# Softmax over 4096 rows of 32768: the last two tiles' stores moved to SyncE's DMA queue, stores in whole rows

One core of one Trainium2 chip. The metric is the device time of one execution in microseconds (us); the profile's span, which begins with the first instruction, is some 2 us shorter.

## The reference

```python
logits: (16, 256, 32768) float32, temperature = 1.0
scaled = logits / temperature
scaled = scaled - scaled.max(axis=-1, keepdims=True)
exp_scaled = np.exp(scaled)
return exp_scaled / exp_scaled.sum(axis=-1, keepdims=True)
```

537 MB are read and 537 MB written, each once.

## The kernel before

Each row of 32768 is cut into two halves on two neighbouring partitions, so a tile is 128 x 16384 floats (8.39 MB, 64 KB per partition), and there are G = 64 tiles, numbered 0 to 63, in three buffers. Loads are issued by SyncE (`nc.sync`), stores by ScalarE (`nc.scalar`). Each has one hardware DMA queue of its own in the profile, q1 (SyncE) and q10 (ScalarE), with 536.9 MB each; I call them the rings. Both feed the same sixteen DMA engines: in the trace, rows of both stand back to back. A transfer of a tile is 128 rows, eight for each DMA engine. The code is shortened here; the whole kernel follows below.

```python
def load(t):
    n = _END if t in (0, G - 1) else _LOAD        # 4096 or 16384 columns
    for s in range(0, W, n):
        nc.sync.dma_start(out=buf[t % _BUFS][:, s : s + n], in_=x[...])

def store(t, a, b):
    n = _END if t >= G - _FINE_STORES else b - a  # _FINE_STORES = 3
    for s in range(a, b, n):
        nc.scalar.dma_start(out=o[...], in_=buf[t % _BUFS][:, s : s + n])

def normalise(t):
    for k in range(K):                            # pieces of the tile
        nc.vector.tensor_reduce(out=nm[:, k], in_=xc, op=max, negate=True)
        nc.scalar.activation(out=xc, in_=xc, func=Exp, bias=nm[:, k], accum_out=ssum[:, k])
    ...                                           # combine maxima and sums: f = factor of each piece
    for k in range(K):
        nc.vector.tensor_scalar_mul(...)          # part of the piece
        nc.scalar.activation(..., func=Copy, scale=f[:, k])   # the rest of it
        if t == G - 1:
            store(t, a, c)                        # last tile: four stores, as pieces are done
    if 0 < t < G - 1:
        store(t, 0, W)

for t in range(_BUFS):
    load(t)
for t in range(G):
    normalise(t)
    if t and t + _BUFS - 1 < G:
        load(t + _BUFS - 1)
```

The program order is kept. Waits are added when it is built: a buffer is reloaded only when its store has landed, and all transfers share eight completion semaphores in turn. So tile 63's load waits for tile 60's store, and a transfer can also wait for an earlier one that used its semaphore.

Of the kernel before, what the change touches and what calls it, by code (L numbers as in the profile page):

```python
# [1 line left out]

# [4 lines left out]


_SPLIT = 2
_BUFS = 3  # L10
_LOAD = 16384
_PIECES = (4096, 4096, 4096, 2048, 2048)
_ON_DVE = (4096, 4096, 2048, 0, 0)
_END = 4096
_END_ON_DVE = 2560
_FINE_STORES = 3
_SETS = 3


@with_exitstack  # L20
def kernel(
    ctx: ExitStack,
    tc: tile.TileContext,
    logits: bass.AP,
    temperature: bass.AP,
    out: bass.AP,
):
    nc = tc.nc
    inv_t = 1.0 / float(temperature)
    P = nc.NUM_PARTITIONS  # L30
    fp32 = mybir.dt.float32
    Exp = mybir.ActivationFunctionType.Exp
    Copy = mybir.ActivationFunctionType.Copy
    X = mybir.AxisListType.X
    A = mybir.AluOpType

    xf = logits.flatten_outer_dims()
    of = out.flatten_outer_dims()
    N, V = xf.shape
    W = V // _SPLIT  # L40
    assert sum(_PIECES) == W and len(_PIECES) == len(_ON_DVE)
    x = xf.rearrange("n (h v) -> (n h) v", h=_SPLIT)
    o = of.rearrange("n (h v) -> (n h) v", h=_SPLIT)
    G = N * _SPLIT // P
    assert G * P == N * _SPLIT
    n_rounds = _SPLIT.bit_length() - 1
    K = max(len(_PIECES), W // _END)

    pool = ctx.enter_context(tc.tile_pool(name="fixed", bufs=1))
    buf = [pool.tile([P, W], fp32, tag=f"x{b}", name=f"x{b}") for b in range(_BUFS)]  # L50
    widths = dict(nm=K, ssum=K, ee=K, f=K, ttj=K, nMh=2, Sh=2, rS=1)
    stat = [
        {
            k: pool.tile([P, w], fp32, tag=f"{k}{s}", name=f"{k}{s}")
            for k, w in widths.items()
        }
        for s in range(_SETS)
    ]

    def load(t: int) -> None:  # L60
        n = _END if t in (0, G - 1) else _LOAD
        for s in range(0, W, n):
            nc.sync.dma_start(  # L63
                out=buf[t % _BUFS][:, s : s + n],
                in_=x[t * P : (t + 1) * P, s : s + n],
            )

    def store(t: int, a: int, b: int) -> None:
        n = _END if t >= G - _FINE_STORES else b - a
        for s in range(a, b, n):  # L70
            nc.scalar.dma_start(  # L71
                out=o[t * P : (t + 1) * P, s : s + n],
                in_=buf[t % _BUFS][:, s : s + n],
            )

    def combine(v, op) -> None:
        for j in range(n_rounds):
            mask = [i ^ (1 << j) for i in range(32)]
            nc.vector.stream_shuffle(  # L79
                out=v[:, j + 1 : j + 2], in_=v[:, j : j + 1], mask=mask  # L80
            )
            nc.vector.tensor_tensor(  # L82
                out=v[:, j + 1 : j + 2],
                in0=v[:, j : j + 1],
                in1=v[:, j + 1 : j + 2],
                op=op,
            )

    def normalise(t: int) -> None:
        xs = buf[t % _BUFS]  # L90
        if t in (0, G - 1):
            sizes = [_END] * (W // _END)
            on_dve = [_END_ON_DVE] * len(sizes)
        else:
            sizes, on_dve = _PIECES, _ON_DVE
        K = len(sizes)
        at = [sum(sizes[:k]) for k in range(K)]
        st = stat[t % _SETS]
        nm, ssum, ee, f, ttj = (st[k][:, :K] for k in ("nm", "ssum", "ee", "f", "ttj"))
        nMh, Sh, rS = st["nMh"], st["Sh"], st["rS"]  # L100
        for k in range(K):
            xc = xs[:, at[k] : at[k] + sizes[k]]
            nc.vector.tensor_reduce(  # L103
                out=nm[:, k : k + 1], in_=xc, axis=X, op=A.max, negate=True
            )
            if inv_t != 1.0:
                nc.vector.tensor_scalar_mul(
                    out=nm[:, k : k + 1], in0=nm[:, k : k + 1], scalar1=inv_t
                )
            nc.scalar.activation(  # L110
                out=xc,
                in_=xc,
                func=Exp,
                bias=nm[:, k : k + 1],
                scale=inv_t,
                accum_out=ssum[:, k : k + 1],
            )
            if t == 1 and k == 0:

                store(0, 0, W)  # L120
        nc.vector.tensor_reduce(out=nMh[:, 0:1], in_=nm, axis=X, op=A.min)  # L121
        combine(nMh, A.min)
        nc.scalar.activation(  # L123
            out=ee, in_=nm, func=Exp, bias=nMh[:, n_rounds : n_rounds + 1], scale=-1.0
        )
        nc.vector.tensor_tensor_reduce(  # L126
            out=ttj,
            in0=ee,
            in1=ssum,
            scale=1.0,  # L130
            scalar=0.0,
            op0=A.mult,
            op1=A.add,
            accum_out=Sh[:, 0:1],
        )
        combine(Sh, A.add)
        nc.vector.reciprocal(out=rS, in_=Sh[:, n_rounds : n_rounds + 1])  # L137
        nc.vector.tensor_scalar_mul(out=f, in0=ee, scalar1=rS)  # L138
        for k in range(K):
            a, b, c = at[k], at[k] + on_dve[k], at[k] + sizes[k]  # L140
            if b > a:
                nc.vector.tensor_scalar_mul(  # L142
                    out=xs[:, a:b], in0=xs[:, a:b], scalar1=f[:, k : k + 1]
                )
            if c > b:
                nc.scalar.activation(  # L146
                    out=xs[:, b:c], in_=xs[:, b:c], func=Copy, scale=f[:, k : k + 1]
                )
            if t == G - 1:
                store(t, a, c)  # L150
        if 0 < t < G - 1:
            store(t, 0, W)

    with tc.manual_schedule():
# [8 lines that stand above are left out]
# [1 line left out]
_INS = ['logits', 'temperature']  # L164
_OUTS = [((16, 256, 32768), 'float32')]

_NUMBERS = {'temperature': 1.0}


# [26 lines left out]
```

## Time and profile before

| | before |
|---|---|
| time, median of three runs | 2496.59 us (2495.63 to 2496.76) |
| span of the profiled run | 2493.4 us |
| VectorE (DVE) / ScalarE (ACT) busy | 63% / 55% |
| moved by DMA | 1073.9 MB, 431 GB/s over the span |

The prediction shows the lines. "GB/s" and "DMA" give one entry for each fortieth of the span. In a chain, each line is start, duration and what ran. In a timeline, `[12.54 <-DMA ...]` is the idle time before the line and what ended it; ACTq and SPq are an engine's DMA-issuing instructions.

One reading goes beyond these views. For each transfer the trace also records sixteen completions, one for each DMA engine, and for each row the start and duration on its engine. They don't name the engine, but a row that follows another on its engine begins 3 to 4 ns before that one ends, so a chain of rows can be followed. I call the engine that completes last the **late engine**.

### The profile page before, as it was taken

What the parts mean: (1) busy time and instruction counts of PE and PEld (TensorE: products, weight loads), DVE (VectorE), ACT (ScalarE), POOL (GpSimd) and SP (SyncE); (2) the same over time, 40 slices, a digit from 0 to 9 for tenths busy, and PEclk for the clock granted to TensorE, in tenths of its full rate; (3) what the DMA queues carried; (4) which work ended last, traced back from release to release, by engine and by line L of the source; (5) the groups of instructions that cost most, each with busy time, mean ns of one, the idle gap of its engine ahead of it and who ended that gap; (6) DMA issues with size and microseconds to landing.
All of it is one profiled execution on the core that took longest, in us unless ns stands there. A gap on an engine that the chain in (4) does not pass through costs nothing.

```text
span 2493.4 us, 2622 instructions
## 1 busy us (share of the span) xinstructions
DVE 1575.8 (63%) x1216; ACT 1367.7 (55%) x895; POOL 0.2 (0%) x4
## 2 busy tenths in 40 slices
DVE  6575665766657666575665755657656566575665
ACT  6464645646556465464554645546455464554654
POOL 0000000000000000000000000000000000000000
DMA  9999999999999999999999999999999999999998
GB/s 421 433 424 436 435 437 424 436 434 437 424 436 435 437 424 436 433 428 435 434 430 433 434 436 427 433 436 431 429 435 437 423 435 437 427 431 437 425 429 379
DMA packets 20612, 1073.91 MB, mean 431 GB/s; under 512 B 2288, under 2 KB 2288, under 8 KB 2288
## 3 DMA queue, kind: packets, MB, share of 16 engines
q10 hardware_dynamic: 10512, 536.88, 49.9%
q1 hardware_dynamic: 10080, 536.88, 49.9%
q14 instruction: 20, 0.16, 0.0%
HBM read 536.87 MB, written 536.87 MB: 431 GB/s over the span
## 4 chain that ended last, share of the span: by engine, by line
DMA 75%; DVE 15%; ACT 9%; issue 0%; SPq 0%; DVEq 0%; ACTq 0%
DMA x<-in_logits_dram 38%; DMA out_dram<-x 37%; DVE nm L103 11%; ACT x L110 7%; DVE x L142 3%; ACT x L146 2%; DVE f L138 0%; SPq L63 0%; ACT ee L123 0%; DVE rS L137 0%; DVE Sh L82 0%; DVE ttj L126 0%; DVE Sh L79 0%; DVEq L191 0%; ACTq L71 0%
## 5 line engine op out<-in xcount | busy, mean ns | idle before, releaser
L103 DVE TENSOR_REDUCE nm<-x 128x1 f32<-128x4096 f32 x318 | 1117.5, 3579 | 678.0 <-DMA x<-in_logits_dram 678.0
L110 ACT ACTIVATE x<-x,nm 128x4096 f32<-128x4096 f32 x318 | 965.3, 3036 | 1026.2 <-DVE nm L103 1013.6
L146 ACT ACTIVATE x<-x,f 128x2048 f32<-128x2048 f32 (+1 forms) x194 | 371.2, 1975 | 75.4 <-DVE f L138 74.1
L142 DVE TENSOR_SCALAR x<-x,f 128x4096 f32<-128x4096 f32 (+2 forms) x194 | 372.2, 1975 | 2.5 <-DVE f L138 0.2
L126 DVE CUSTOM_DVE_ANT_0 ttj<-ee,ssum 128x5 f32<-128x5 f32 (+1 forms) x64 | 10.6, 166 | 203.0 <-ACT ee L123 203.0
L110 ACT ACTIVATION_READ_ACCUMULATOR x<-x,nm 128x1 f32 x318 | 59.2, 186 | 0.0
L123 ACT ACTIVATE ee<-nm,nMh 128x5 f32<-128x5 f32 (+1 forms) x64 | 18.1, 283 | 0.0
L138 DVE TENSOR_SCALAR f<-ee,rS 128x5 f32<-128x5 f32 (+1 forms) x64 | 14.8, 231 | 2.2
L137 DVE RECIPROCAL rS<-Sh 128x1 f32<-128x1 f32 x64 | 10.5, 164 | 2.2
L82 DVE TENSOR_TENSOR nMh<-nMh 128x1 f32<-128x1 f32 x64 | 10.2, 160 | 2.2
L82 DVE TENSOR_TENSOR Sh<-Sh 128x1 f32<-128x1 f32 x64 | 10.2, 159 | 2.2
L121 DVE TENSOR_REDUCE nMh<-nm 128x1 f32<-128x5 f32 (+1 forms) x64 | 10.1, 157 | 2.2
L79 DVE STREAM_SHUFFLE nMh<-nMh 128x1 f32<-128x1 f32 x64 | 9.7, 151 | 0.0
L79 DVE STREAM_SHUFFLE Sh<-Sh 128x1 f32<-128x1 f32 x64 | 9.7, 151 | 0.0
L110 ACT ACT_TABLE_LOAD x1 | 1.3, 1283 | 8.1 <-DMA x<-in_logits_dram 8.1
L126 DVE DVE_READ_ACCUMULATOR2_ANT Sh<- 128x1 f32 x64 | 5.3, 83 | 0.0
L79 DVE LOAD_MASK_SELECT Sh<-Sh x64 | 0.9, 14 | 2.8
L79 DVE LOAD_MASK_SELECT nMh<-nMh x64 | 0.9, 14 | 2.8
L177 POOL MEMSET const-bfloat16-1.0<- 128x1 bf16 x1 | 0.1, 101 | 0.0
L177 POOL MEMSET const-uint8-127<- 128x1 uint8 x1 | 0.1, 101 | 0.0
L177 POOL MEMSET const-float32-0.0<- 128x1 f32 x1 | 0.1, 98 | 0.2 <-issue 0.2
L177 POOL MEMSET const-float32-1.0<- 128x1 f32 x1 | 0.1, 98 | 0.0
## 6 DMA issues: line engine op xcount, KB each, us to landing
out_dram<-x ACTq DMA_DIRECT2D x12, 2048.0 KB, 19.3
x<-in_logits_dram SPq DMA_DIRECT2D x8, 2048.0 KB, 18.4
x<-in_logits_dram SPq DMA_DIRECT2D x62, 43.6
out_dram<-x ACTq DMA_DIRECT2D x61, 44.3
```

Of the source, the lines that this page charges most:

```text
L79: nc.vector.stream_shuffle(out=v[:, j + 1 : j + 2], in_=v[:, j : j + 1], mask=mask)
L82: nc.vector.tensor_tensor(out=v[:, j + 1 : j + 2], in0=v[:, j : j + 1], in1=v[:, j + 1 : j + 2], op=op,)
L103: nc.vector.tensor_reduce(out=nm[:, k : k + 1], in_=xc, axis=X, op=A.max, negate=True)
L110: nc.scalar.activation(out=xc, in_=xc, func=Exp, bias=nm[:, k : k + 1], scale=inv_t, accum_out=ssum[:, k : k + 1],)
L121: nc.vector.tensor_reduce(out=nMh[:, 0:1], in_=nm, axis=X, op=A.min)
L123: nc.scalar.activation(out=ee, in_=nm, func=Exp, bias=nMh[:, n_rounds : n_rounds + 1], scale=-1.0)
L126: nc.vector.tensor_tensor_reduce(out=ttj, in0=ee, in1=ssum, scale=1.0, scalar=0.0, op0=A.mult, op1=A.add, accum_out=Sh[:, 0:1],)
L137: nc.vector.reciprocal(out=rS, in_=Sh[:, n_rounds : n_rounds + 1])
L138: nc.vector.tensor_scalar_mul(out=f, in0=ee, scalar1=rS)
L142: nc.vector.tensor_scalar_mul(out=xs[:, a:b], in0=xs[:, a:b], scalar1=f[:, k : k + 1])
L146: nc.scalar.activation(out=xs[:, b:c], in_=xs[:, b:c], func=Copy, scale=f[:, k : k + 1])
L177: nc = _bacc.Bacc("TRN2", target_bir_lowering=False, num_devices=1)
```

## The change

The intent: the last load should not share DMA time with a store that is less urgent, ScalarE should not issue (and wait for) stores while its arithmetic is on the critical path, and stores should use the largest rows.

```diff
-_FINE_STORES = 3
 ...
     def store(t: int, a: int, b: int) -> None:
-        n = _END if t >= G - _FINE_STORES else b - a
-        for s in range(a, b, n):
-            nc.scalar.dma_start(
-                out=o[t * P : (t + 1) * P, s : s + n],
-                in_=buf[t % _BUFS][:, s : s + n],
-            )
+
+        engine = nc.sync if t >= G - 2 else nc.scalar
+        engine.dma_start(
+            out=o[t * P : (t + 1) * P, a:b], in_=buf[t % _BUFS][:, a:b]
+        )
```

In effect: tile 61's store becomes one 8 MB transfer on ScalarE's ring instead of four of 2 MB; tile 62's becomes one on SyncE's ring, behind tile 63's load; tile 63's four go to SyncE's ring. Nothing else changes.

## The prediction

> **What bounds the kernel now.** I read the page first (slices, chain of work that ended last), then the end of the span as chain, timeline and windows, because the change touches only the stores of the last three tiles. There are 64 tiles of 128 x 16384 floats (8.39 MB), numbered 0 to 63; three buffers.
>
> ```profile
> DMA  9999999999999999999999999999999999999998
> GB/s 421 433 424 436 435 437 424 436 434 437 424 436 435 437 424 436 433 428 435 434 430 433 434 436 427 433 436 431 429 435 437 423 435 437 427 431 437 425 429 379
> DMA 75%; DVE 15%; ACT 9%; issue 0%; SPq 0%; DVEq 0%; ACTq 0%
> ```
>
> The DMA engines are full in every slice but the last, and the chain is three quarters DMA. 1073.9 MB in 2493.4 us is 431 GB/s; from 100 to 2400 us the windows give 433 GB/s. Neither number of bytes nor middle changes, so all that can be won is idle time of the DMA engines at the end. The windows over the end (window, length, DVE busy, ACT busy, POOL busy, clock, DMA share, GB/s) show how much that is:
>
> ```profile
> 2460.00:2465.00 5.00, 0.00 (x0) 5.00 (x5) 0.00 (x0) 1.00 1.02 436
> 2465.00:2470.00 5.00, 0.98 (x8) 3.85 (x4) 0.00 (x0) 1.00 0.25 108
> 2470.00:2475.00 5.00, 5.00 (x4) 4.03 (x3) 0.00 (x0) 1.00 0.63 264
> 2475.00:2480.00 5.00, 0.83 (x1) 2.05 (x2) 0.00 (x0) 1.00 0.99 419
> ```
>
> From 2465 to 2475 the engines are idle for 5 x 0.75 + 5 x 0.37 = 5.6 us on average: tile 62's store is out and tile 63's is not yet ready. The chain and ScalarE's timeline name the cause:
>
> ```profile
> 2411.84 41.26 DMA x<-in_logits_dram
> 2453.10 0.02 issue
> 2453.12 0.02 ACTq L71
> ...
> 2453.18 0.34 ACTq L71
> 2453.51 0.05 issue
> 2453.56 14.87 ACT x L110 x8
> ```
>
> ```profile
> 2439.82 13.70 ACTq L71 DMA_DIRECT2D out_dram<-x  x3
> 2453.56 3.71 ACT L110 ACTIVATE x<-x,nm 128x4096 f32<-128x4096 f32 x1 [12.54 <-DMA x<-in_logits_dram]
> ```
>
> ScalarE issues tile 62's last quarter store only at 2453.18, just after tile 63's last quarter load landed at 2453.10, and only then starts tile 63's exponentials, although VectorE had the first maximum at 2440.89 + 4.37 = 2445.3. The wait lists of the built program explain it: all transfers share eight completion semaphores in turn, and the four stores of tile 62 have the semaphores of the four loads of tile 63, so each waits for that load. ScalarE works in order, so its arithmetic waits as well. It then needs 14.87 us back to back, 2453.56 to 2468.4.
>
> **What the Trainium skill says.** (1) "DMA: Bandwidth & Descriptors", section Queues, rings and completion order: each DMA engine goes round robin between the rings that have work, packet by packet. The trace agrees, and shows that a packet here is one row of one transfer (20612 packets = 143 transfers x 128 rows, + 143 x 16 completions): with 64 KB rows on both rings the load lands some 5.0 us after the store that ended before it (2371.3 to 2376.3), with 16 KB store rows against 64 KB load rows 3.07 us after (2409.94 to 2413.01). (2) Same page, Issuing engines are not separate DMA queues: issuing from another engine adds no bandwidth. Agrees so far: loads alone at the start take 19.35 us per tile (22.69 to 42.04), 433 GB/s, as much as loads and stores together. (3) Same page, Where 436 GB/s comes from: a ceiling of 435.2 GB/s; the 433 of the middle is at it. (4) Same page, Why a DMA increments its semaphore by 16 and not by 1: the sixteen engines finish independently. The trace shows that this decides the case: it has sixteen completions per transfer, and for tile 62's last quarter store the first came at 2466.0, the median at 2466.2, the fifteenth at 2468.3 and the last at 2470.7. One engine is 4.7 us behind the rest, as it is all through the kernel. The average idle time above is mostly that of the other fifteen.
>
> **The change part by part.**
> Removed: eight 2 MB stores by ScalarE (tiles 61, 62) and four more (tile 63); added: one 8 MB store by ScalarE (61), one 8 MB and four 2 MB stores by SyncE. An issue costs 0.34 us in the timeline. For tiles before 61 nothing differs: VectorE's order is the same, and their stores already were 8 MB.
>
> *ScalarE is freed.* With no store of tile 62 in its order, it can start on tile 63 with the first maximum. In the new wait lists nothing in the last two tiles waits for a load that has not long landed.
>
> *Tile 62 lands later.* Store 61 now has 64 KB rows, so the rest of load 62 goes at half rate rather than at four fifths: it lands 5.0 us after 2409.94, at 2415.0, not at 2413.0. VectorE's 17.46 us of maxima, the normalisation and the maxima of tile 63 are back to back from there, so tile 63's maxima end at 2458.3 + 2.0 = 2460.3. ScalarE's fourth exponential then runs 2460.3 to 2464.1, and from the next instruction to the first store issue it took 2471.52 - 2468.34 = 3.2 us before, so tile 63's first store is issued at about 2467.3, against 2471.52: 4.2 us earlier.
>
> *Does load 63 come in time?* Its rows stay 16 KB against store 61's 64 KB, so it now gets one fifth. On the slowest engine: a 64 KB row takes 19.35/8 = 2.42 us, a 16 KB row 4.89/8 = 0.61 us (quarter loads at the start landed 4.89 us apart). From about 2413.5, seven pairs take 7 x 3.03 = 21.2 us, to 2434.7; the remaining 25 rows of the load 15.3 us, to 2450.0. With 1.4 us to the completion its quarters land at about 2436.7, 2441.6, 2446.5 and 2451.4. VectorE wants them at 2442.9, 2447.3, 2451.7 and 2456.1: 4.7 us of room for the last, so it stays in VectorE's shadow.
>
> *The DMA engines at the end.* Store 62 follows load 63 on SyncE's ring. The slowest engine moves its eight rows from 2450.0 in 19.4 us, to 2469.4: the same moment as before (landing 2470.7 less 1.4), as it must be, since it has the same bytes and was never idle. Before, it then stood still until the first packets of tile 63, about 2471.9; now tile 63's store has been waiting since 2467.3. So its idle 2.5 us go, and no more, although the first issue comes 4.2 us earlier and the average engine loses 5.6 us of idle time less. Tile 63's four stores then take 4 x 4.89 = 19.6 us: 2489.0, landing 2490.4, against 2492.5. **Sum: about 2.1 to 2.3 us less, span 2491.2; time 2496.6 - 2.3 = 2494.3 us (0.1%).**
>
> **The rivals.**
> (a) *All idle time goes.* If the lag of the slow engine is made by the sharing of 16 KB rows (its skew on store 61's quarters is 9.6 us, against about 7 in the middle) and is smaller after the change, the end is set by the first issue, 4.2 us earlier, or by the 5.6 us of mean idle time: 2491 to 2492.4. For it: the other fifteen engines would be ready. Against: a lag of this size is there from 400 us on with 64 KB rows as well.
> (b) *Load 63 starves.* If an engine takes several large rows before it changes rings, or the slowest engine lags on the load's side as well, the last quarter could land after 2456 and the wait for the load would take the place of the removed one: each further microsecond moves the first store, with 2 us to spare, so 2494 to 2497. Against: the 3.07 us above fits one row by turns (0.61 + 2.42 = 3.03).
> (c) *Nothing gained.* SyncE is slower to see two engines' results than ScalarE is to follow its own, or the one long store at the end drains no better: 2496 to 2497. SyncE is otherwise idle, so I give it little.
> (d) *A bound that was shifted to SyncE's ring.* Store 62 behind the load on one ring, with no other ring busy, could run slower than on two. Loads alone ran at 433 GB/s, so I expect no loss.
>
> **Range and chances.** The middle is the slow engine's sum, 2494.3. Rival (a) sets the low side, (b) and (c) the high side, and the runs before spread over 1.1 us by themselves. Range 2491.8 to 2496.2. Two per cent would be 50 us; the whole idle time at the end is 5.6 us, and a loss of 50 us would be more than two tiles' transfer. So within 2%: 0.98, and 0.01 for either side.
>
> **What would show it.** Right: no ScalarE queue wait in the last two tiles; VectorE starts tile 62 at about 2415 and tile 63's maxima end near 2460.3; ScalarE's exponentials of tile 63 begin near 2447.3; first store of tile 63 issued near 2467.3; windows from 2465 to 2475 nearly full; tile 62's store landing near 2470.7 with one engine late; span near 2491.2. Wrong: a VectorE wait on tile 63's load; a slow engine that is no longer late (then more is won); an issue of the last stores after 2469.4; or any difference before 2400 us, which the change gives no reason for.

## The result

| | time, median (all runs) | against before |
|---|---|---|
| before, same rounds | 2496.21 us (2495.63 to 2496.76, 4 runs) | |
| changed | 2495.38 us (2492.81 to 2498.45, 4 runs) | 0.9997 [0.998, 1.0015] |

The ratio is not quite the ratio of the medians; the brackets are the 95% interval. The profiled run happened to be the slowest of the four, with a span of 2496.7 us, 3.3 us longer than that of before.

The page of the changed kernel, its DMA slices and the chain by engine:

```profile
DMA  9999999999999999999999999999999999999998
GB/s 419 436 429 430 433 437 436 435 437 426 434 434 437 433 426 435 434 436 423 433 433 433 435 425 436 436 433 425 435 422 436 421 437 436 421 436 422 436 429 380
DMA 73%; DVE 16%; ACT 9%; another core or an unknown queue 2%; issue 0%; SPq 0%; DVEq 0%; ACTq 0%
```

Still DMA from end to end; the last slice went from 379 to 380 GB/s. The chain has 2% on a queue that it can't name; its list in order of time stops at 2475.2 us, where only tile 63's stores are left. Now the windows of the end (window, length, DVE, ACT, POOL busy, clock, DMA share, GB/s):

```profile
2460.00:2465.00 5.00, 4.44 (x5) 4.48 (x3) 0.00 (x0) 1.00 1.15 498
2465.00:2470.00 5.00, 1.62 (x8) 3.85 (x4) 0.00 (x0) 1.00 0.64 275
2470.00:2475.00 5.00, 5.00 (x4) 5.00 (x4) 0.00 (x0) 1.00 0.76 316
2475.00:2480.00 5.00, 0.20 (x1) 0.12 (x1) 0.00 (x0) 1.00 0.99 423
```

Idle time on average is 5 x 0.36 + 5 x 0.24 = 3.0 us, against 5.6. ScalarE, SyncE and VectorE in their timelines, and the chain:

```profile
2451.02 3.71 ACT L108 ACTIVATE x<-x,nm 128x4096 f32<-128x4096 f32 x1 [4.33 <-DVE nm L101]
```

```profile
2446.73 0.35 SPq L70 DMA_DIRECT2D out_dram<-x  x1
...
2470.88 0.34 SPq L70 DMA_DIRECT2D out_dram<-x  x1
```

```profile
2418.69 17.46 DVE L101 TENSOR_REDUCE nm<-x 128x1 f32<-128x4096 f32 x5 [10.50 <-DMA x<-in_logits_dram]
...
2446.58 17.39 DVE L101 TENSOR_REDUCE nm<-x 128x1 f32<-128x4096 f32 x4
```

```profile
2440.85 5.81 DVE x L140 x3
2446.66 17.32 DVE nm L101 x4
2463.98 0.02 issue
2464.00 3.80 ACT x L108 x2
```

ScalarE now starts tile 63 as soon as the first maximum is there, without a wait for a DMA and without an issue in between. VectorE runs the four maxima without a gap, so the load came in time. In the chain the end of that load and ScalarE's queue are gone: it goes from VectorE straight to the last exponential. The first store of tile 63 is issued at 2470.88.

Absolute times of the two traces can't be compared here: tile 60's store, in which the programs do not differ yet, landed at 2409.94 before and at 2413.84 now. From there on:

| us after the late engine's completion of tile 60's store | before | changed |
|---|---|---|
| tile 62 loaded | 3.0 | 4.8 |
| first store of tile 63 issued | 61.6 | 57.0 |
| late engine completes tile 62's store | 60.8 | 62.2 |
| late engine completes tile 63's first store | 67.9 | 67.1 |
| all complete | 82.6 | 81.6 |

So the change wins about 1 us in the tail in this pair of traces, although the first store was issued 4.5 us earlier, and a stretch that it doesn't touch lost 3.9 us.

Who is left at the end? The windows of before from 2491, and of the changed kernel from 2492:

```profile
2491.00:2492.00 1.00, 0.00 (x0) 0.00 (x0) 0.00 (x0) 1.00 0.61 262
2492.00:2493.00 1.00, 0.00 (x0) 0.00 (x0) 0.00 (x0) 1.00 0.01 0
```

```profile
2492.00:2493.00 1.00, 0.00 (x0) 0.00 (x0) 0.00 (x0) 1.00 0.08 33
2493.00:2494.00 1.00, 0.00 (x0) 0.00 (x0) 0.00 (x0) 1.00 0.08 33
2494.00:2495.00 1.00, 0.00 (x0) 0.00 (x0) 0.00 (x0) 1.00 0.04 16
```

One engine of sixteen is a share of 0.06. Before, all sixteen stop together. Now fifteen are done by 2492.1 and one works alone for three microseconds more; its completion comes 3.6 us after the median one.

### The profile page after: what moved, and what is told of

The parts are those of the page before. It is cut to its first block, busy times and chain, and to the rows that moved or that the text cites. A ratio compares the mean times of both kernels' runs of the same rounds, so it can differ in the third digit from the quotient of the medians.

```text
span 2496.7 us, 2616 instructions
## 1 busy us (share of the span) xinstructions
DVE 1575.6 (63%) x1216; ACT 1367.8 (55%) x895; POOL 0.2 (0%) x4
## 4 chain that ended last, share of the span: by engine, by line
DMA 73%; DVE 16%; ACT 9%; another core or an unknown queue 2%; issue 0%; SPq 0%; DVEq 0%; ACTq 0%
DMA x<-in_logits_dram 37%; DMA out_dram<-x 36%; DVE nm L101 12%; ACT x L108 7%; DVE x L140 3%; ACT x L144 2%; DVE f L136 0%; ACT ee L121 0%; DVE rS L135 0%; DVE Sh L80 0%; DVE ttj L124 0%; DVE Sh L77 0%; SPq L62 0%; DVEq L189 0%
## 5 line engine op out<-in xcount | busy, mean ns | idle before, releaser
L135 DVE RECIPROCAL rS<-Sh 128x1 f32<-128x1 f32 x64 | 10.5, 164 | 2.2
L119 DVE TENSOR_REDUCE nMh<-nm 128x1 f32<-128x5 f32 (+1 forms) x64 | 10.1, 158 | 2.2
```

Of the source, the lines that this page charges most:

```text
L119: nc.vector.tensor_reduce(out=nMh[:, 0:1], in_=nm, axis=X, op=A.min)
L135: nc.vector.reciprocal(out=rS, in_=Sh[:, n_rounds : n_rounds + 1])
```

## The experiments

Two theories at first. **The late engine:** the end is set by the DMA engine that is behind, so only its idle time between tile 62's store and tile 63's is won. **The first issue:** the end is set by when tile 63's store is first issued, or by the average engine. All runs returned correct results. The runs of a group shared a chip and the runs of before. Edits are against the kernel before unless said otherwise.

### First group: the changed kernel again, and its parts

Before in these rounds: median 2496.16 us, but 2494.05 to 2504.27 in 11 runs.

**after_again.** No edit.

> The changed kernel again, with more rounds. Theory A (the engine that lags sets the end; only its idle time between tile 62's store and tile 63's first store is won, 2.3 us): the mean over the rounds is 1.5 to 3 us below the kernel before, and in the trace the slowest engine completes tile 63's first quarter store 4.8 to 4.9 us after tile 62's store (no idle time), where it was 7.2 us before. The scatter of 2492.8 to 2498.5 us seen so far comes from slow packets before the last three tiles, so single runs of both kernels should scatter by some microseconds. Rival B (the first issue or the mean idle time counts): 4 to 6 us below. Rival C (nothing won): 0, and the larger scatter belongs to the change.

Measured: 2499.54 us median (2495.67 to 2501.78, 6 runs), ratio 1.0004 [0.999, 1.0018]. No win in the time; the scatter belongs to both kernels. In the trace the late engine completes tile 63's first store 4.6 us after tile 62's: no idle time. So the mechanism is there, and the sum is not.

**scalar_whole.** Whole rows, but all stores by ScalarE:

```diff
-_FINE_STORES = 3
+_FINE_STORES = 0
```

> Whole 8 MB stores of tiles 61 and 62, but all issued by ScalarE: one part of the change alone. Packet-by-packet sharing (theory A): tile 62's store starts on ScalarE's ring at about 2443 us beside tile 63's load and its 64 KB rows take four fifths; the load's last quarter lands near 2470 instead of 2451, VectorE waits some 14 us for it, the first store of tile 63 is issued near 2482, and the span is 2503 to 2506, 10 to 13 us above the kernel before. Rival (the ring does not matter, only that ScalarE does not wait for the load's semaphore): the same as the changed kernel, within 1 us.

Measured: 2511.26 us median (2506.74 to 2519.44, 6 runs), ratio 1.0057 [1.0038, 1.0076], span 2509.8 in the profile. That is more than the 10 to 13 us expected, but in the stretch after tile 60's store alone it is 12 us (last table). VectorE's timeline:

```profile
2447.51 13.06 DVE L103 TENSOR_REDUCE nm<-x 128x1 f32<-128x4096 f32 x3
2476.59 4.42 DVE L103 TENSOR_REDUCE nm<-x 128x1 f32<-128x4096 f32 x1 [16.01 <-DMA x<-in_logits_dram]
```

VectorE waits 16.0 us for the last quarter of tile 63's load, and it waits for the late engine alone: the median engine completed that quarter at 2454.4 and the fifteenth at 2457.4, both before VectorE was free at 2460.6, and the last at 2476.6. No store of tiles 61 and 62 waits for that load in this build, yet the kernel is 0.6% slower than before. It differs from the changed kernel in the ring of the last two tiles' stores alone. So the ring is what counts for whole rows: behind the load on SyncE's ring the store can't take its turns; beside it, on the engine that still has load rows left, it takes most of the time.

**scalar_62_fine.** Tile 61's store whole, 62's in quarters, by ScalarE:

```diff
-        n = _END if t >= G - _FINE_STORES else b - a
+        n = _END if t >= G - 2 else b - a
```

> Tile 61's store whole, tile 62's in four quarters, all by ScalarE: this alone moves the completion semaphores, so that ScalarE no longer waits for tile 63's load before its arithmetic. Theory A: ScalarE's queue wait goes, but tile 62's 16 KB rows share with the load row by row from about 2440 on, so its last quarter lands near 2461, VectorE waits about 5 us for it, the first store of tile 63 is issued near 2472.5 as before the change, and the time is 0 to 2 us above the kernel before. Rival (the semaphore wait was all): the same as the changed kernel, 2 us below before.

Measured: 2498.95 us median (2494.98 to 2505.97, 6 runs), ratio 1.0006 [0.9989, 1.0023]. VectorE's timeline:

```profile
2443.28 13.06 DVE L103 TENSOR_REDUCE nm<-x 128x1 f32<-128x4096 f32 x3
2461.21 4.42 DVE L103 TENSOR_REDUCE nm<-x 128x1 f32<-128x4096 f32 x1 [4.87 <-DMA x<-in_logits_dram]
```

Predicted: the last quarter near 2461, a wait of about 5 us, the first store of tile 63 near 2472.5. Measured: 2461.2, 4.87 us, 2472.56. Taking the semaphore wait from ScalarE gains nothing by itself; VectorE's wait for the load takes its place. The late engine is idle before tile 63 again (6.45 us between its two completions).

**sync_fine.** SyncE's ring, but 16 KB rows:

```diff
         n = _END if t >= G - _FINE_STORES else b - a
+        engine = nc.sync if t >= G - 2 else nc.scalar
         for s in range(a, b, n):
-            nc.scalar.dma_start(
+            engine.dma_start(
```

> The other part alone: tiles 62 and 63 stored by SyncE, but tiles 61 and 62 still in 16 KB rows. Theory A: tile 62 lands 2 us earlier than in the changed kernel and the first store of tile 63 is issued 2 us earlier, but the slowest engine is busy without a gap in both, so the time is that of the changed kernel within 1 us, 1.5 to 3 us below before. Rival (the first issue sets the end): 2 us below the changed kernel. Rival (64 KB rows are what helps): the same as before.

Measured: 2493.31 us median (2492.18 to 2496.44), ratio 0.9983 [0.9968, 0.9998]: the only one of this group below before, and 6.2 us below the changed kernel's median in the same rounds. Neither theory had said so much. It could be chance before the tail, or a cost of whole rows. That was open.

### Second group: chance or cost, and the issue delayed

Before: median 2496.24 us (2493.22 to 2500.33, 11 runs).

**after_3.** No edit to the changed kernel.

> The changed kernel a third time, beside the all-SyncE fine version on one chip. Open after the first runs: it came out 5 us above the fine version and 1 us above the kernel before, though its trace has no idle time on the late engine. Theory A2 (inside the last three tiles it wins about 1 us over before and loses 0.8 us to the fine version; the rest is slow packets before tile 61, where the programs are the same, so chance): over these rounds the mean lies 0 to 2 us below before and within 2 us of the fine version. Rival (whole stores of tiles 61 and 62 cost 4 us in some way each time): again 4 to 6 us above the fine version and at or above before.

**sync_fine_2.** No edit to sync_fine.

> The fine version again: stores of 62 and 63 by SyncE, 16 KB rows. Theory A2: 1.5 to 3 us below before. If its first 4 us were real: 3 to 5 us below before.

Measured: after_3 2496.64 us (2492.71 to 2505.59), ratio 1.0004 [0.9989, 1.002]; sync_fine_2 2498.68 us (2490.98 to 2513.79), ratio 1.0015 [0.9993, 1.0038]. The order of the two has turned round. So the gap of the first group was almost all chance, and so was sync_fine's win; the expectation of 1.5 to 3 us below before is missed as well. Times of six runs can't resolve two microseconds here.

**delay_3** and **delay_8.** Against sync_fine: a ScalarE copy of 4624 or 10586 columns, on a buffer that is no longer used, ahead of tile 63's scaling:

```diff
+        if t == G - 1:
+            spare = buf[(G - 3) % _BUFS][:, :4624]     # delay_8: 10586
+            nc.scalar.activation(out=spare, in_=spare, func=Copy)
         for k in range(K):
```

> The fine version with an idle ScalarE copy that delays tile 63's four stores by 3 us. Theory A (the latest engine sets the end; it finishes tile 62's rows some 5 us after the first issue in the fine version): no loss, within 1 us of the fine version, and in the trace still 4.8 to 4.9 us between the late engine's completion of tile 62's last store and of tile 63's first. Rival B (the first issue or the mean engine sets the end): 3 us more than the fine version, and all sixteen engines complete together.

> The same with 8 us of delay, beyond what the late engine hides. Theory A: the first store is issued near 2473.6, the late engine stands idle for 3 to 3.5 us, so 3 to 4 us above the fine version, and all engines complete together to 0.2 us. Rival B: 8 us above the fine version.

Measured: delay_3 2494.75 us (2491.44 to 2500.48, 6 runs), ratio 0.9995 [0.9982, 1.0009]; delay_8 2499.73 us (2497.34 to 2507.86, 4 runs), ratio 1.0018 [1.0002, 1.0034]. Beside sync_fine_2's median of the same rounds that is 3.9 us less and 1.1 us more, so neither theory's times came true, and with this scatter the times decide nothing. The traces, one of each, do. From tile 60's store to the issue of tile 63's first store, sync_fine takes 55.3 us in both its traces, delay_3 57.8 and delay_8 62.8, so the delays came out as 2.5 and 7.5 us. From tile 60's store to the last completion sync_fine takes 80.9 us in both its traces. delay_3 takes 81.0 us, and the late engine's two completions are 4.95 us apart: no idle time. delay_8 takes 84.4 us, 3.5 more, and the completions are 7.52 us apart. Of the 3.5 us, 2.7 are this gap (3 to 3.5 were expected); the other 0.8 lie in the last three stores, where one engine ended 0.7 us after the rest. delay_8's windows at that place:

```profile
2480.00:2485.00 5.00, 0.38 (x1) 5.00 (x4) 0.00 (x0) 1.00 0.15 62
2485.00:2490.00 5.00, 0.00 (x0) 2.95 (x3) 0.00 (x0) 1.00 1.02 429
```

The average engine is idle 85% of the first five microseconds, and still only 3.5 of the 7.5 us are lost. The late engine hides the rest. This decides for the late engine.

### Third group: the kernel before, for its tail

> The kernel before once more, for its trace. In the one trace so far the late engine's completion of tile 60's store is 82.6 us before the last completion of all; in three traces of the changed kernel it is 81.4 to 81.6. If the change wins 1 us in the tail, this trace shows 82.2 to 83 us again, with the late engine idle for 2 to 3 us between tile 62's store and tile 63's first; and the span less the mean extra time of slow packets is about 2483, against 2482.4 in the changed kernel. If 82.6 was chance, it shows 81.5 or less, or above 83.5.

> The same again, with the same expectations: two more looks show how far the tail of one and the same program scatters, apart from the stretch before it.

No edit in either. One look each: 2501.81 and 2495.92 us (before beside them 2498.32), state unknown, so only the traces are used. before_3 fits its expectation; before_2's 82.0 us of tail is just under the range of 82.2 to 83, and the late engine's idle time was 1.4 us (6.26 less 4.9), also under it.

### All traces together

"Extra" is by how much rows took longer than the usual 2.418 us (64 KB) or 0.611 us (16 KB), summed and divided by sixteen. "Tail" is from the late engine's completion of tile 60's store to the last completion. "Apart" is between the late engine's completions of tile 62's last and tile 63's first store; 4.9 is without a gap.

| run | span | extra | span less extra | tail | apart |
|---|---|---|---|---|---|
| before | 2493.4 | 10.5 | 2482.9 | 82.6 | 7.16 |
| before_2 | 2499.7 | 16.8 | 2482.9 | 82.0 | 6.26 |
| before_3 | 2493.8 | 10.1 | 2483.7 | 82.4 | 6.96 |
| changed | 2496.7 | 14.4 | 2482.3 | 81.6 | 4.84 |
| after_again | 2497.0 | 14.6 | 2482.4 | 81.5 | 4.63 |
| after_3 | 2498.7 | 16.3 | 2482.4 | 81.4 | 4.84 |
| sync_fine | 2492.1 | 10.7 | 2481.4 | 80.9 | 4.83 |
| sync_fine_2 | 2495.0 | 13.0 | 2482.0 | 80.9 | 4.87 |
| delay_3 | 2491.7 | 9.6 | 2482.1 | 81.0 | 4.95 |
| delay_8 | 2506.1 | 20.6 | 2485.5 | 84.4 | 7.52 |
| scalar_62_fine | 2494.7 | 11.1 | 2483.6 | 83.1 | 6.45 |
| scalar_whole | 2509.8 | 15.3 | 2494.5 | 94.3 | 18.34 |

Spans of one and the same program differ by 6.3 us (before), and slow rows account for nearly all of it: less the extra they lie within 0.8 us. With that taken off, three traces of each agree: the tail is 82.3 us before and 81.5 in the changed kernel on average, the span less extra 2483.2 and 2482.4. The ranges of the tails, 82.0 to 82.6 and 81.4 to 81.6, do not overlap. **The change wins 0.8 to 0.9 us.** sync_fine, with delay_3, whose delay is hidden, wins another 0.5 to 0.6 us; in the time that is lost in the scatter. So no version here beats the kernel before by an amount that its times show. What makes a row slow was not tested and stays open.

Where the other microsecond went: with means of three traces, before's late engine completes tile 62's store 60.9 us after tile 60's, the changed kernel's after 62.2, so 1.3 us later. Then it wins 2.0 us (6.8 to 4.8 apart) and 0.2 us in the last three stores.

The 1.3 us have two parts. The first is a transfer of the profile's instruction queue (8 KB, 0.309 us), which I take for an instruction fetch. In the changed kernel's three traces it stands back to back, within 4 ns, behind a row of tile 62, 1 to 4 us before the late engine completes that tile. In the first and third, the row after it begins as it ends and takes 2.768 us in place of 2.418; in the second, it falls behind the tile's last row, and tile 63's first row takes 0.958 in place of 0.611. So 0.31 + 0.35 = 0.66 us, of which only the 0.31 come before tile 62's completion in the second trace. In the kernel before, the same fetch comes at 2470.58, 2477.29 and 2471.00, near the end of tile 62's store, and no row follows it: it fell into the idle time that the change takes away.

The second part shows when the late engine is followed back row by row. In the last quarter of tile 63's load, when it serves that load alone, one or two rows took 0.70, 0.53 and 0.69 us too long in the three traces (rows at 2453.71 and 2454.84; 2454.19 and 2454.95; 2455.72). In the three traces of before, no row after tile 60's store is slow by more than 0.11 us. Together that is 1.2 us on average, of 1.3. sync_fine and its three relatives have the fetch in tile 62's store too, but 16 KB rows; they complete it after 61.5 to 61.6 us, 0.7 later than before, which is the fetch alone. So the slow rows came with whole rows here; why they are slow is not shown.

Why one engine is late was not tested. By their timing, fetches are part of it: in the trace of before, at eight of them between 365 and 2189 us, the fetch and the slowed row behind it cost 0.84 to 0.87 us together, and the late engine's distance from the median engine grew by 0.8 to 1.0 us on the store that ended next. Between them it shrank again.

## Why the prediction was right, and where its steps were off

The measured median is 1.1 us above the predicted 2494.3 and inside the range, and "within 2%" is right. But the time can't tell 2.3 us from nothing, so the steps have to be judged by the traces. Times below count from tile 60's store, 2409.94 in the prediction and 2413.84 in the first trace of the changed kernel.

- *ScalarE is freed:* right. No DMA wait of ScalarE from 2410 on, where it was 12.5 us.
- *Tile 62 lands later, 5.0 us after:* 4.8. Right, with the turns row by row behind it.
- *Load 63 comes in time,* last quarter at 2451.4, so 41.5 us after: 42.1, and VectorE did not wait. Right to 0.7 us; the slow rows above are the difference.
- *First store of tile 63 at 2467.3,* 57.4 us after: 57.0. Right.
- *Only the late engine's idle time is won:* right, and shown by the two delays. Rival (a), that all idle time goes, is refuted by them; (b) did not come about, while scalar_whole shows what starving the load costs; of (c), the times show no gain, but its reason did not come true, because SyncE issued the first store at 57.0 us, not late; (d) showed no sign: store 62's rows took their usual 2.418 us on a ring alone.
- *"the same moment as before (landing 2470.7 less 1.4), as it must be, since it has the same bytes and was never idle":* **the step that failed in size.** The late engine completed tile 62 1.3 us later, because up to 0.66 us of instruction fetch and the row slowed by it, free before in the gap, now stood in its work, and rows of load 63's last quarter were 0.5 to 0.7 us slow. That term was taken as zero. Also, the idle time was 1.9 us in the mean of three traces (6.8 less 4.9), not 2.5: in the trace that was read, the last row of tile 62 ended at 2470.37, not 2469.4 (its completion followed 0.3 us later, not 1.4), and the first of tile 63 began at 2472.50, not 2471.9. The sum is 0.9 us instead of 2.3.
- *The spread of 1.1 us over the runs before:* far too small, being three runs. With more rounds before alone spans 2493.2 to 2504.3. The range was right with luck: two of the four runs lie within 0.01 us of its high end or above it (2496.19 and 2498.45), and the medians of later rounds, 2499.54 and 2496.64, lie above it.
- *"any difference before 2400 us, which the change gives no reason for"* would make it wrong, I wrote. There was one, 3.9 us; in the traces it comes with slow rows, and before_2 shows the same in the unchanged program.
- *Windows from 2465 to 2475 nearly full* was to show it right: they were 0.64 and 0.76 full, and 0.59 and 0.98 when moved by the 3.9 us (2468.9 to 2473.9 and 2473.9 to 2478.9). The sign did not follow from the mechanism, which leaves the other engines idle until the first store is issued.
- *"One engine is 4.7 us behind the rest", "as it is all through the kernel":* 4.7 us is from the first engine's completion; from the median it was 4.5 us there and 6.4 to 7.9 us on the stores from 393 to 2410 us. And the 20612 packets include 20 of the instruction queue; the two products give 20592.

## What to carry to other kernels

When the DMA engines are full, ask not how long they idle on average but how long the engine that is last idles: completions for each engine tell, and here it was a third of the average (1.9 us against 5.6). Where a late load and a store share the engines, the ring and the row size decide which is served. Put the store behind the load on the same ring; with the store on the other ring VectorE waited 16.0 us for the load when the rows were whole and still 4.9 us when they were quarters. And where chance is larger than the effect, measure a stretch within the trace from a common event, in several traces, rather than the whole time.

## What the Trainium skill lacked or had wrong

- "DMA: Bandwidth & Descriptors", section Queues, rings and completion order, puts a turn at some 9 to 17 descriptors. How many descriptors a row is, no trace shows, but here a turn is one row of a transfer, of 16 or 64 KB. Followed row by row, the late engine of the kernel before takes the 16 KB rows of load 63 and store 61 one by one in turn, 0.607 us apart; and the sums fit: 0.61 + 2.42 = 3.03 us for one of each, and in the kernel before tile 62's load landed 3.0 us after tile 60's store. In the changed kernel, with a 64 KB row on each ring (2 x 2.42 = 4.84 us), it landed 4.8 us after. The page doesn't say that unequal rows so divide the engines unequally: scalar_whole's VectorE waited 16.0 us.
- Same page, Rules for kernel authors: spreading transfers over issuing engines only saves issue time. For the total rate no run contradicts it. What the page lacks is that the ring of a store sets the order in which load and store are served: scalar_whole and the changed kernel differ in that alone, and their tails are 94.3 and 81.5 us.
- The same page says that the engines finish independently, but not how far apart. Here the last was 4.5 to 6.2 us behind the median on the next-to-last tile's store, in every kernel.
- No page gives the cost of an instruction fetch to a full DMA engine; it belongs to "Runtime: NRT & Kernel Launch", section Instruction fetch mechanics. Here it was 0.309 us, and 0.13 to 0.64 us more for the row right behind it (0.35 in tile 62's store).
- None gives the scatter of row times: 10 to 21 us of extra per engine over a span, from run to run of one program 10.1 to 16.8.
